# One tile pair instead of two for the keeping jobs, coarse pool waits outside the attention, and seven block products in group 0 of the second MLP

## The chip, the cores and the metric

The kernel runs on one core of a Trainium2 chip. The metric is the device time of one execution in microseconds (us); before and after are medians of several runs.

## The reference, cut to what matters

A decoder trunk of two layers on x (1 x 1024 tokens x 1024 channels, float32). Layer 0 mixes with a diagonal state-space block (S5) and a gated projection (GLU), layer 1 with 16-head stick-breaking attention over keys and values computed from the residual stream. Each layer ends with the same kind of MLP, and every sub-layer has a pre-norm whose shift, scale and gate come from a conditioning vector c:

```python
x = x + g_a[:, None, :] * mix
h = modulate(rms_norm(x, mlp_norm_g[i]), sh_m, sc_m)
ff = einsum('bsf,fd->bsd', square(relu(einsum('bsd,df->bsf', h, mlp_w1[i]))), mlp_w2[i])
x = x + g_m[:, None, :] * ff
```

with D = 1024 and D_FF = 4096. The modulations are matrix-vector products with c: `ada_chunks(c, ada_w, ada_b, n)`.

## The kernel before, in words

**Products.** Every float32 product is made from a high part (`uh`, `hi`, type fp32r) and the rest (`ul`, `lo`): three matmuls of 128x128 by 128x512, `mm3` (lines 247 to 253). A weight unit of 128x1024 is loaded by SP into one of three `raw` buffers (`load_unit`, line 209), cast to `uh` by ACT (line 217), and `ul` is the difference, on DVE (line 84 through `sub`).

**An MLP** (`mlp`, line 916) takes the 4096 hidden rows in 8 groups c of 4 blocks j. `ups` (line 1044) computes a block for both halves h of the tokens: 24 matmuls each, relu on ACT (line 927) into a tile `ra` or `rb`, the square on DVE. In group 0 the blocks are made half by half instead (lines 1052 to 1060), since the second half's norm is computed meanwhile. The way back, for one group, is done in one of two ways:
- plain (`down`, line 937): 16 outputs (8 row blocks by two halves), each 4 x 3 matmuls, 192 in all, and one DVE instruction that adds the output to x;
- seven products (`seven`, line 984): the 4 blocks by 2 halves are seen as 2x2 blocks of matrices, and for each of 4 weight units 7 products of 6 matmuls replace 8, 168 in all. `enter` (line 948) makes the right-hand combinations (T1 to T4 and three blocks as they are) with sums and splits on DVE and ACT, into `f` and `e` tiles; `blocks` (line 966) makes the left-hand ones, mostly on POOL; the results are added to x on DVE.

`fast(c)` says which way is taken: in the second MLP (layer 1) groups 1 to 7 go by seven products, group 0 plain. The first MLP is plain throughout.

**Side jobs of the GLU and of the first MLP.** `mid` (line 1635) takes 3 or 4 jobs from a list after every fourth of a down stage and after every block of an up stage. Two kinds:
- `gemv` (line 174): one 128-row piece of a modulation. SP loads 512 KB into a `raw` buffer, DVE multiplies it by silu(c) and sums (line 177, shown as CUSTOM_DVE_ANT_0). It shares the three `raw` buffers with the weights.
- `keep` (line 224): half a unit of a later weight (the output, the K/V and the query projections) is split ahead of time and put into DRAM, for the attention to load without any work. All of it is issued by POOL: load `raw` (line 231), for K/V and queries the product with the norm's scale (line 78), cast to `hi` (line 236), difference in place (line 84), two stores `kh` and `kl` (line 239). 64 jobs of 512 columns; two pairs of tiles `e` (raw, hi) are used in turn, by the half c:

```python
        while len(keeps) < 4:
            keeps.append(fs0.extra((F32, F32R)[len(keeps) % 2]))
        raw, hi = keeps[0:2] if c == 0 else keeps[2:4]
        G.dma_start(raw, src[:, cs])
```

**Order.** Side jobs are listed two gemv to one keep. The framework orders each engine's instructions with a timeline simulation when it compiles, and the engines then run them in that order, each waiting on semaphores; inside S5 and for TensorE in the attention the order is fixed by hand.

**Pools.** Tiles lie in pools that open and close along the kernel. A pool opened on bytes of closed ones has either coarse waits (each of its tiles waits for every user of those pools) or, with `reuse_waits="tile"` (`tile_pool`, line 95), waits of each tile for the users of its own bytes alone. Before, all pools opened by this helper have the fine form. Pools that land on closed ones: those after S5 (`pax0`, `fpa`, `fpe`, `gp`), `fpb` after the GLU, the attention's own (`atp`, `atk`, `aq`, `pz`, `ppt`, `ppo`, and `late`), and those after the attention (`xp1`, `raw1`, `pax1` and the second `Inner`'s).

**After the attention** the rest of its output projection runs (`oproj`, line 1672), the residual is read back into 16 `x` tiles (line 1665), and the second MLP follows to the end of the kernel.

Of the kernel before, what the change touches and what calls it, by code (L numbers as in the profile page):

```python
# [8 lines left out]
F32 = mybir.dt.float32  # L9
F32R = mybir.dt.float32r  # L10
# [4 lines left out]
PSUM = bass.MemoryType.PSUM  # L15
DRAM = bass.MemoryType.DRAM

P = 128
# [3 lines left out]
HN = 512  # L22
# [34 lines left out]
def kernel(ctx, tc, A, out):  # L57
# [4 lines left out]
    class Engine:  # L62
        def __init__(self, eng):
            self.eng = eng
# [12 lines left out]
    def mul(o, a, b, eng=V):  # L77
        eng.tensor_tensor(o, a, b, op=ALU.mult)  # L78
# [4 lines left out]
    def sub(o, a, b, eng=V):  # L83
        eng.tensor_tensor(o, a, b, op=ALU.subtract)  # L84
# [10 lines left out]
    def tile_pool(name, bufs=1, **k):  # L95
        return tc.tile_pool(name=name, bufs=bufs, reuse_waits="tile", **k)
# [6 lines left out]
    pools, turns = {}, {}  # L103

    def open_x(i):
        es = ExitStack()
        pools["x"] = es.enter_context(tile_pool(f"xp{i}", bufs=16 if i else 1))
        pools["raw"] = es.enter_context(tile_pool(f"raw{i}", bufs=3))
        es.callback(pools.pop, "raw")
        turns.clear()  # L110
        return es

    def open_ax(i):
        es = ExitStack()
        pools["ax"] = es.enter_context(tile_pool(f"pax{i}", bufs=4 if "pv" in pools else 6, space=PSUM))
        return es

    cnt = [0]
# [1 line left out]
    def nm(s):  # L120
        cnt[0] += 1
        return f"{s}_{cnt[0]}"
# [7 lines left out]
    def ps_mm(shape=(P, HN)):  # L130
        return pmm.tile(list(shape), F32, tag="mm", name=nm("pm"))

    def open_pv():
        es = ExitStack()
        pools["pv"] = es.enter_context(tile_pool("ppv", bufs=2, space=PSUM))
        es.callback(pools.pop, "pv")
        return es

# [40 lines left out]
    def ada_chunk(c0, after=None):  # L179
        def one(i):  # L180
            gemv(A["adaT"][i - 16], silr, mod[:, i:i + 1])

        def fin():
            add(mod[:, c0:c0 + 8], mod[:, c0:c0 + 8], adab[:, c0:c0 + 8])
            if after is not None:
                after()

        return [(lambda i=i: one(i)) for i in range(c0, c0 + 8)] + [fin]
# [7 lines left out]
    def queue(jobs, n, others):  # L196
        while jobs or others:
            side.extend(jobs[:n] + others[:1])
            del jobs[:n], others[:1]

    def scale_cols(n, sc0):
        stt(scl[:, 8 * n:8 * n + 8], mod[:, sc0:sc0 + 8], 1.0, gcol[:, 8 * n:8 * n + 8],
            ALU.add, ALU.mult)
# [5 lines left out]
    def load_unit(src):  # L209
        raw = raw_tile()  # L210
        SP.dma_start(raw, src)
        return split_unit(raw)
# [9 lines left out]
    kept, keeps = {}, []  # L222

    def keep(key, src, c, scale=None):
        if c == 0:
            kept[key] = [dp.tile([P, 1024], F32, name=nm(name)) for name in ("kh", "kl")]
        cs = slice(HN * c, HN * c + HN)
        while len(keeps) < 4:
            keeps.append(fs0.extra((F32, F32R)[len(keeps) % 2]))
        raw, hi = keeps[0:2] if c == 0 else keeps[2:4]  # L230
        G.dma_start(raw, src[:, cs])
        if scale is not None:
            nk = scale.shape[1] // 2
            r3 = raw.rearrange("p (k m) -> p k m", k=nk)
            mul(r3, r3, scale[:, nk * c:nk * c + nk].unsqueeze(2).broadcast_to([P, nk, HN // nk]), G)
        G.tensor_copy(hi, raw)
        sub(raw, raw, hi, G)
        for d, t in zip(kept[key], (hi.bitcast(F32), raw)):
            G.dma_start(d[:, cs], t)
# [7 lines left out]
    def mm3(ps, u, j, hl, first, last):  # L247
        uh, ul = u
        sl = slice(j * 128, j * 128 + 128)
        hi, lo = hl  # L250
        T.matmul(ps, uh[:, sl], hi, start=first, stop=False)  # L251
        T.matmul(ps, uh[:, sl], lo, start=False, stop=False)  # L252
        T.matmul(ps, ul[:, sl], hi, start=False, stop=last)  # L253
# [7 lines left out]

    def s5(hook):
        es = ExitStack()
        sp = es.enter_context(tile_pool("sp", bufs=1))
        pp = es.enter_context(tile_pool("s5ps", bufs=2, space=PSUM))

        cst = sp.tile([P, C_N], F32, name="cst")
        SP.dma_start(cst, A["cst"])
# [279 lines left out]
        class Block:  # L548
# [165 lines left out]
            pv, vt = None, None  # L714
# [163 lines left out]
    class Inner:  # L878


        def __init__(self):
            self.n, self.pools, self.es = 0, {}, {}

        def open(self, name):
            self.es[name] = ExitStack()
            self.pools[name] = self.es[name].enter_context(tile_pool("fp" + name))

        def close(self, *names):
            for name in names:
# [9 lines left out]
            return self.pools["e"].tile([P, HN], dt, tag="e", name=nm("e"), bufs=8)  # L899

        def raw(self, tag):
            return self.pools["b"].tile([P, HN], F32, tag=tag, name=nm(tag), bufs=2)

    def norm_tiles(fs):
        spare = {}

        def norm_tile(tag, bufs):
            n = spare.setdefault(tag, [0, []])
            n[0] += 1
            if len(n[1]) < bufs:  # L910
                n[1].append(fs.tile(F32))
            return n[1][(n[0] - 1) % bufs]

        return norm_tile

    def mlp(layer, xs, hs, norm, fs, mid=None, done=None, place=None):
# [3 lines left out]
        hid, raws = {}, {}  # L920

        def up(f, u, h, tag="ra"):
            p = ps_mm()
            for k in range(8):
                mm3(p, u, k, hs[k][h], k == 0, k == 7)
            r = fs.raw(tag)
            ACT.activation(r, p, AF.Relu)  # L927
            mul(r, r, r)
            return r

        def halves(r, wide=False):
            hi, lo = f_tile(wide=wide), f_tile(wide=wide)
            ACT.copy(hi, r)
            sub(lo, r, hi)
            return hi, lo
# [97 lines left out]
        def plain(c, j, h, r):  # L1033
            raws[j, h] = r
            if c and j == 0:
                return
            if c and (j, h) == (2, 0):
                hid[0, 0], hid[0, 1] = halves(raws[0, 0]), halves(raws[0, 1])
            hid[j, h] = halves(r)

        def fast(c):
            return layer == 1 and c > 0

        def ups(c, j):
            u = load_unit(w1[4 * c + j])
# [6 lines left out]
        for h in range(2):  # L1052
            for f in range(4):
                u = load_unit(w1[f])
                plain(0, f, h, up(f, u, h))
                if h == 0 and f == 0:
                    norm.rstd(1)
                elif h == 0 and f == 1:
                    norm.spread(1)
                    norm.apply(1, 0, 8)  # L1060
        for c in range(8):
# [4 lines left out]
            elif c < 7:  # L1066
                for op in range(4):
                    u = load_unit(w2[c, op])
# [5 lines left out]
            else:  # L1074
                for h in range(2):
                    for op in range(4):
                        u = load_unit(w2[c, op])
# [405 lines left out]
        return oh, ou[-2:]  # L1483


    pools["un"] = ctx.enter_context(tile_pool("unp", bufs=3))
    x_es = open_x(0)
    xall = pools["x"].tile([P, 16, HN], F32, name="xall")
    pv_es = open_pv()
    ada_es = ExitStack()  # L1490
    rowp = ada_es.enter_context(tile_pool("rowp", bufs=1))
    silr = rowp.tile([P, D], F32, name="silr")

    def gate(i):
# [27 lines left out]
    fs = fs0 = Inner()  # L1522
    fs.open("a")
    fs.open("e")
    norm = Norm(norm_tiles(fs), xs, hs, 2, M_SHM0)
    with tile_pool("gp", bufs=1) as gp:
        queue(ada_chunk(M_SHM0) + ada_chunk(M_SCM0, lambda: scale_cols(2, M_SCM0)) + ada_chunk(M_GM0), 2,
              [(lambda i=i, c=c: keep(("o", i), A["wo"][i], c)) for i in range(8) for c in range(2)])

        def glu(i, ug, uv, h):  # L1530
            ps = ps_pv if h == 1 and i <= 5 else ps_mm
            pg, pv = ps(), ps()
            for k in range(8):
                mm3(pg, ug, k, ys[k][h], k == 0, k == 7)
            if (i, h) == (6, 1):
                norm.spread(0)
                norm.apply(0, 0, 8)
            for k in range(8):
                mm3(pv, uv, k, ys[k][h], k == 0, k == 7)
            g = gp.tile([P, HN], F32, tag="g", name=nm("g"), bufs=3)  # L1540
            ACT.activation(g, pg, AF.Sigmoid)
            mul(g, pv, g)
            stt(xs[i][h], g, mod[:, M_GA0 + i:M_GA0 + i + 1], xs[i][h], ALU.mult, ALU.add)
            norm.square(i, h)

        for i in range(6):
            ug, uv = first if i == 0 else (load_unit(A["wglu"][8 + i]), load_unit(A["wglu"][i]))
            for h in range(2):
                glu(i, ug, uv, h)
                if i == 0:  # L1550
                    for c in range(1 + 3 * h, 4 + 4 * h):
                        gate(c)
            if i:
                pump(9)
        for h in range(2):
            for i in range(6, 8):
                ug = load_unit(A["wglu"][8 + i])
                uv = load_unit(A["wglu"][i])
                glu(i, ug, uv, h)
            if h == 0:  # L1560
                norm.rstd(0)
# [100 lines left out]
    for h in range(2):  # L1662
        for k in range(8):
            xs2[k][h] = xt()
            SP.dma_start(xs2[k][h], xd[k][h])
    fs = Inner()
    for name in "aeb":
        fs.open(name)
        ctx.enter_context(fs.es[name])
# [117 lines left out]
```

## Time and profile before

| | us |
|---|---|
| median of 3 runs | 2519.15 |
| lowest, highest run | 2518.10, 2522.58 |
| the profiled execution | 2516.43 |
| its span, first to last instruction | 2514.7 |
| TensorE (PE) busy | 2350.6 (93%) |
| VectorE (DVE) busy | 1754.3 (70%) |
| GpSimd (POOL) busy | 909.5 (36%) |

The profiled execution lies 2.7 us below the median. The stages in the span: S5 to about 240 us, the GLU to about 410, the first MLP to about 1130, the attention to about 1793, the rest of its projection and the second MLP to the end. PE is the TensorE matmul row; a single matmul is shown longer than the distance to the next one, since they overlap, so a stage's matmuls are counted and divided into its time. An answer with "<-" names what ended an idle time.

### The profile page before, as it was taken

How to read it: one execution, taken by the hardware profiler on the slowest of the kernel's cores; microseconds unless marked ns; L12 is line 12 of the kernel's file. 1: busy time of each engine (PE TensorE's matmuls, PEld its weight loads, DVE VectorE, ACT ScalarE, POOL GpSimd, SP SyncE). 2: the span in 40 equal slices, each digit the busy share in tenths (PEclk: the TensorE clock that was granted, in tenths of full speed). 3: DMA queues.
4: the chain of work that ended last, by engine and by line, in shares of the span. 5: the costliest groups of instructions: out<-in, count | busy, mean ns of one | idle time of the engine just before them, and what ended most of it. 6: DMA issues, size and time to landing. Idle time of an engine off the chain costs nothing.

```text
span 2514.7 us, 33271 instructions
## 1 busy us (share of the span) xinstructions
PE 2350.6 (93%) x12552; PEld 1979.3 (79%) x12552; DVE 1754.3 (70%) x2570; ACT 941.8 (37%) x1710; POOL 909.5 (36%) x965
## 2 busy tenths in 40 slices
PE   3888999989999999999899999998999999999998
PEld 2677788867778888888888888887778888888886
DVE  7997557766776545345687877788583667876787
ACT  5653124211111222133566666676351232223221
POOL 4664460378775000014333323343110322342334
PEclk8899999999999999998999999999999999999999
DMA  4225863667766333123211111126721011111112
GB/s 150 86 79 188 283 221 105 216 241 251 252 239 217 101 117 126 45 89 102 81 58 39 64 68 68 59 100 213 250 78 57 34 51 59 60 42 51 56 54 76
DMA packets 105344, 297.08 MB, mean 118 GB/s; under 512 B 13280, under 2 KB 25568, under 8 KB 105184
## 3 DMA queue, kind: packets, MB, share of 16 engines
q1 hardware_dynamic: 87264, 240.42, 27.9%
q0 software_dynamic: 15360, 50.34, 5.5%
q10 hardware_dynamic: 2560, 4.20, 0.7%
q8 instruction: 99, 1.62, 0.3%
q14 instruction: 61, 0.50, 0.1%
HBM read 241.23 MB, written 49.48 MB: 116 GB/s over the span
## 4 chain that ended last, share of the span: by engine, by line
PE 61%; DVE 17%; DMA 11%; issue 5%; ACT 2%; POOL 1%; SPq 0%; DVEq 0%; POOLq 0%; ACTq 0%
DMA raw<-in_adaT_dram 8%; PE pm L70 8%; PE pm L251 8%; PE pm L252 8%; PE pm L253 8%; PE pa L1001 3%; PE pa L999 3%; PE pa L1000 3%; PE pt L70 3%; DVE sn L1282 3%; DVE raw L177 2%; PE pa L253 2%; PE pa L251 2%; PE pa L252 2%; PE po L70 2%
## 5 line engine op out<-in xcount | busy, mean ns | idle before, releaser
L251 PE MATMUL pm<-h,uh 128*128 128x512 f32 x1192 | 465.6, 393 | 19.3 <-ACT rb L927 15.8
L253 PE MATMUL pm<-h,ul 128*128 128x512 f32 x1192 | 465.5, 391 | 4.7 <-DVE ul L84 4.7
L252 PE MATMUL pm<-h,uh 128*128 128x512 f32 x1192 | 466.3, 391 | 1.6 <-DVE h L93 1.6
L217 ACT CAST uh<-raw 128x1024 fp32r<-128x1024 f32 x130 | 136.7, 1051 | 486.9 <-PE pa L252 154.5
L84 DVE TENSOR_TENSOR ul<-raw,uh 128x1024 fp32r<-128x1024 f32 (+1 forms) x158 | 202.7, 1283 | 126.5 <-ACT uh L217 103.8
L251 PEld LDWEIGHTS pm<-h,uh 128*128 128x128 f32 x1192 | 225.0, 189 | 71.5 <-ACT rb L927 19.3
L177 DVE CUSTOM_DVE_ANT_0 raw<-raw,silr 128x1024 f32<-128x1024 f32 x119 | 162.5, 1369 | 155.4 <-DMA raw<-in_adaT_dram 140.6
L253 PEld LDWEIGHTS pm<-h,ul 128*128 128x128 f32 x1192 | 225.1, 189 | 52.5 <-DVE ul L84 5.6
L252 PEld LDWEIGHTS pm<-h,uh 128*128 128x128 f32 x1192 | 225.3, 189 | 48.6 <-DVE h L93 2.2
L70 PE MATMUL pm<-uh,h 128*128 128x256 f32 x1024 | 238.5, 301 | 3.8 <-DVE rs L1138 3.0
L1282 DVE TENSOR_TENSOR_SCAN sn<-sn 128x768 f32<-128x768 f32 (+7 forms) x128 | 180.6, 1417 | 46.5 <-ACT sn L1277 45.2
L81 POOL TENSOR_TENSOR f<-f,f 128x512 f32<-128x512 f32 x30 | 44.0, 1468 | 397.3 <-ACT f L831 397.2
L70 PEld LDWEIGHTS pm<-uh,h 128*128 128x128 f32 x1024 | 181.7, 199 | 5.0 <-DVE rs L1138 3.4
L81 POOL TENSOR_TENSOR raw<-raw 128x256 f32<-128x256 f32 x28 | 26.0, 929 | 411.4 <-DVE ul L84 411.4
L251 PE MATMUL pa<-f,uh 128*128 128x512 f32 x396 | 154.4, 390 | 1.7 <-DVE xall L93 1.0
L252 PE MATMUL pa<-f,uh 128*128 128x512 f32 x396 | 154.1, 389 | 0.0
L253 PE MATMUL pa<-f,ul 128*128 128x512 f32 x396 | 153.7, 389 | 0.0
L70 PE MATMUL pm<-ul,h 128*128 128x256 f32 x512 | 148.7, 290 | 0.9 <-DMA ul<-kl 0.9
L78 POOL TENSOR_TENSOR sg<-sg,sn 128x512 f32<-128x512 f32 x64 | 93.0, 1453 | 122.5 <-DVE sn L1282 56.3
L70 PE MATMUL pm<-h,uh 128*128 128x512 f32 x402 | 133.7, 414 | 0.0
L93 DVE SCALAR_TENSOR_TENSOR x<-pa,mod,x 128x512 f32<-128x512 f32 x143 | 103.3, 743 | 43.5 <-PE pa L253 29.6
L1277 ACT ACTIVATE sn<-z,rrr 128x512 f32<-128x512 f32 (+1 forms) x192 | 111.6, 581 | 46.9 <-PE z L70 45.4
(380 smaller groups left out, 5497.7 us busy)
## 6 DMA issues: line engine op xcount, KB each, us to landing
raw<-in_w_dram SPq DMA_DIRECT2D x140, 512.0 KB, 3.3
raw<-in_adaT_dram SPq DMA_DIRECT2D x96, 512.0 KB, 3.7
uh<-kh SPq DMA_DIRECT2D x40, 512.0 KB, 4.2
ul<-kl SPq DMA_DIRECT2D x40, 512.0 KB, 4.0
kh<-e POOLq DMA_DIRECT2D x64, 256.0 KB, 2.7
kl<-e POOLq DMA_DIRECT2D x64, 256.0 KB, 3.6
raw<-in_wT_dram SPq DMA_DIRECT2D x24, 512.0 KB, 4.3
raw<-in_wglu_dram SPq DMA_DIRECT2D x20, 512.0 KB, 4.7
```

The lines of the kernel that those rows point to most:

```text
L70: return lambda *a, **k: tc.keep_in_program_order(f(*a, **k))
L78: eng.tensor_tensor(o, a, b, op=ALU.mult)
L84: eng.tensor_tensor(o, a, b, op=ALU.subtract)
L93: V.scalar_tensor_tensor(o, a, s, b, op0=op0, op1=op1)
L177: V.tensor_tensor_reduce(raw, raw, row, 1.0, 0.0, op0=ALU.mult, op1=ALU.add, accum_out=bcol)
L217: ACT.copy(uh, raw)
L251: T.matmul(ps, uh[:, sl], hi, start=first, stop=False)
L252: T.matmul(ps, uh[:, sl], lo, start=False, stop=False)
L253: T.matmul(ps, ul[:, sl], hi, start=False, stop=last)
L999: T.matmul(p, uh[:, sl], hi, start=(i == 0), stop=False)
L1277: ACT.activation(g[:, HN * hb + c0:HN * hb + HN], p[:, c0:], AF.Sigmoid, scale=pj.rr[:, 2, t, a:a + 1])
L1282: V.tensor_tensor_scan(g[:, s0:], g[:, s0:], g[:, s0:], 1.0, op0=ALU.mult, op1=ALU.bypass)
```

## The change

1. `keep` uses one pair of tiles for all jobs.
2. All pools but the attention's (`atp`, `atk`, `aq`, `pz`, `ppt`, `ppo`, `late`) get the coarse waits: `tile_pool(...)` becomes `tc.tile_pool(name=..., ...)`.
3. `fast` is true for all groups of layer 1. Group 0's blocks go through `enter`, in the order of group 0 (four blocks of the first half, then four of the second), and so all eight `ra`/`rb` tiles are alive at once: the second `Inner` gets 4 buffers for each of the two tags.

```diff
-        while len(keeps) < 4:
-            keeps.append(fs0.extra((F32, F32R)[len(keeps) % 2]))
-        raw, hi = keeps[0:2] if c == 0 else keeps[2:4]
+        if not keeps:
+            keeps.extend((fs0.extra(F32), fs0.extra(F32R)))
+        raw, hi = keeps
         G.dma_start(raw, src[:, cs])
...
-        pools["x"] = es.enter_context(tile_pool(f"xp{i}", bufs=16 if i else 1))
-        pools["raw"] = es.enter_context(tile_pool(f"raw{i}", bufs=3))
+        pools["x"] = es.enter_context(tc.tile_pool(name=f"xp{i}", bufs=16 if i else 1))
+        pools["raw"] = es.enter_context(tc.tile_pool(name=f"raw{i}", bufs=3))
...
-        pools["ax"] = es.enter_context(tile_pool(f"pax{i}", bufs=4 if "pv" in pools else 6, space=PSUM))
+        pools["ax"] = es.enter_context(tc.tile_pool(name=f"pax{i}", bufs=4 if "pv" in pools else 6, space=PSUM))
...
-        def __init__(self):
+        def __init__(self, raws=2):
+            self.raws = raws
...
-            self.pools[name] = self.es[name].enter_context(tile_pool("fp" + name))
+            self.pools[name] = self.es[name].enter_context(tc.tile_pool(name="fp" + name, bufs=1))
...
-            return self.pools["b"].tile([P, HN], F32, tag=tag, name=nm(tag), bufs=2)
+            return self.pools["b"].tile([P, HN], F32, tag=tag, name=nm(tag), bufs=self.raws)
...
         def fast(c):
-            return layer == 1 and c > 0
+            return layer == 1
...
                 u = load_unit(w1[f])
-                plain(0, f, h, up(f, u, h))
+                if fast(0):
+                    enter(f, h, up(f, u, h, "ra" if f < 2 else "rb"))
+                else:
+                    plain(0, f, h, up(f, u, h))
...
-    fs = Inner()
+    fs = Inner(4)
```

The pools `ppv`, `sp`, `s5ps`, `unp`, `rowp` and `gp` change like `raw`.

## Rows read from the trace of the kernel before

**Rows 1.** Page, part 1: busy time, share and instructions of each engine.

```profile
PE 2350.6 (93%) x12552; PEld 1979.3 (79%) x12552; DVE 1754.3 (70%) x2570; ACT 941.8 (37%) x1710; POOL 909.5 (36%) x965
```

**Rows 2.** Table by stretch: length, then each engine's busy time and instructions, clock, DMA.

```profile
474.00:800.00 326.00, 306.41 (x1321) 248.58 (x1320) 225.48 (x255) 54.88 (x77) 249.22 (x286) 0.98 0.71 248
800.00:1090.00 290.00, 290.00 (x1297) 240.71 (x1296) 137.88 (x187) 62.93 (x87) 0.00 (x0) 1.00 0.28 95
1900.00:1943.00 43.00, 43.00 (x192) 35.61 (x191) 17.42 (x21) 4.65 (x5) 0.00 (x0) 1.00 0.14 50
1990.00:2080.00 90.00, 90.00 (x399) 74.55 (x398) 67.82 (x91) 24.31 (x36) 31.92 (x28) 1.00 0.16 53
520.00:540.00 20.00, 13.53 (x55) 10.76 (x54) 13.62 (x17) 2.06 (x3) 15.93 (x18) 0.83 0.73 256
```

**Rows 3.** 474 to 800 us: the chain of waits by line, and who waited.

```profile
by line: DMA raw<-in_adaT_dram 49.6%; DVE raw L177 14.5%; DVE ul L84 10.7%; issue 10.0%; DVE xall L93 4.1%; DVE f L84 3.2%; DVE ra L78 1.8%; DVE rb L78 1.2%; ACT f L933 1.2%; DVE mod L177 0.6%; PE pa L251 0.6%; PE pa L252 0.6%; PE pa L253 0
...
DVE raw L177 <- DMA raw<-in_adaT_dram: 86.1, 44, 3.9
...
PE pm L251 <- ACT rb L927: 15.8, 7, 6.5
```

**Rows 4.** DVE groups of instructions: three of 474 to 800 us, three of 900 to 1090.

```profile
L177 DVE CUSTOM_DVE_ANT_0 raw<-raw,silr 128x1024 f32<-128x1024 f32 x54 | 79.6, 1474 | 86.1 <-DMA raw<-in_adaT_dram 86.1
L84 DVE TENSOR_TENSOR ul<-raw,uh 128x1024 fp32r<-128x1024 f32 x27 | 43.7, 1620 | 0.0
L78 DVE TENSOR_TENSOR rb<-rb 128x512 f32<-128x512 f32 x12 | 15.8, 1317 | 0.0
...
L84 DVE TENSOR_TENSOR ul<-raw,uh 128x1024 fp32r<-128x1024 f32 x18 | 22.0, 1224 | 33.3 <-ACT uh L217 32.8
L177 DVE CUSTOM_DVE_ANT_0 raw<-raw,silr 128x1024 f32<-128x1024 f32 x9 | 10.8, 1223 | 6.7 <-DMA raw<-in_wT_dram 5.1 <-ACT silr L1571 1.7
L78 DVE TENSOR_TENSOR rb<-rb 128x512 f32<-128x512 f32 x9 | 6.2, 688 | 12.0 <-ACT rb L927 12.0
```

**Rows 5.** Page, part 6: DMA issues, KB each, median us from issue to landing.

```profile
raw<-in_w_dram SPq DMA_DIRECT2D x140, 512.0 KB, 3.3
raw<-in_adaT_dram SPq DMA_DIRECT2D x96, 512.0 KB, 3.7
...
kl<-e POOLq DMA_DIRECT2D x64, 256.0 KB, 3.6
```

**Rows 6.** POOL's groups of instructions, 474 to 800 us (the keeping jobs).

```profile
L84 POOL TENSOR_TENSOR e<-e,e 128x512 f32<-128x512 f32 x48 | 63.3, 1318 | 1.2
L78 POOL TENSOR_TENSOR e<-e,scl 128x512 f32<-128x512 f32 x48 | 62.8, 1309 | 108.0 <-DVE scl L93 71.6 <-DMA e<-in_wkv_dram 24.6 <-DMA e<-in_wq_dram 11.2
L236 POOL CAST e<-e 128x512 fp32r<-128x512 f32 x48 | 48.4, 1011 | 2.8
```

**Rows 7.** The load of a keeping job (line 231): issue to landing, min/median/max.

```profile
DMA to landing us min/median/max: 2.8/3.6/6.5
```

**Rows 8.** POOL in order of time: first scaled keep, last store, next work.

```profile
474.36 3.43 POOL L78 TENSOR_TENSOR e<-e,scl 128x512 f32<-128x512 f32 x2 [71.62 <-DVE scl L93]
...
795.71 0.54 POOL L239 DMA_DIRECT2D kl<-e  x1
1104.41 1.74 POOL L81 TENSOR_TENSOR f<-f,f 128x512 f32<-128x512 f32 x1 [308.16 <-ACT f L831]
```

**Rows 9.** End of the attention in order of time: SP's queue, then PE.

```profile
1781.35 1.28 SPq L211 DMA_DIRECT2D raw<-in_w_dram  x3
...
1795.38 9.78 SPq L1665 DMA_DIRECT2D x<-xd  x16
...
1792.95 0.39 PE L251 MATMUL pa<-h,uh 128*128 128x512 f32 x1
```

**Rows 10.** PE's waits from 1790 us to the end.

```profile
PE pa L251 <- DVE x L93: 2.9, 1, 2.9
PE pa L999 <- ACT e L933: 2.6, 2, 2.0
```

More of the change, by code (lines that the diff above doesn't have):

```diff
@@ L134, in open_pv @@
         es = ExitStack()
-        pools["pv"] = es.enter_context(tile_pool("ppv", bufs=2, space=PSUM))
+        pools["pv"] = es.enter_context(tc.tile_pool(name="ppv", bufs=2, space=PSUM))
         es.callback(pools.pop, "pv")
@@ L263, in s5 @@
         es = ExitStack()
-        sp = es.enter_context(tile_pool("sp", bufs=1))
-        pp = es.enter_context(tile_pool("s5ps", bufs=2, space=PSUM))
+        sp = es.enter_context(tc.tile_pool(name="sp", bufs=1))
+        pp = es.enter_context(tc.tile_pool(name="s5ps", bufs=2, space=PSUM))
         cst = sp.tile([P, C_N], F32, name="cst")
@@ L1483, in attention @@
         return oh, ou[-2:]
-    pools["un"] = ctx.enter_context(tile_pool("unp", bufs=3))
+    pools["un"] = ctx.enter_context(tc.tile_pool(name="unp", bufs=3))
     x_es = open_x(0)
@@ L1490 @@
     ada_es = ExitStack()
-    rowp = ada_es.enter_context(tile_pool("rowp", bufs=1))
+    rowp = ada_es.enter_context(tc.tile_pool(name="rowp", bufs=1))
     silr = rowp.tile([P, D], F32, name="silr")
@@ L1525 @@
     norm = Norm(norm_tiles(fs), xs, hs, 2, M_SHM0)
-    with tile_pool("gp", bufs=1) as gp:
+    with tc.tile_pool(name="gp", bufs=1) as gp:
         queue(ada_chunk(M_SHM0) + ada_chunk(M_SCM0, lambda: scale_cols(2, M_SCM0)) + ada_chunk(M_GM0), 2,
```

## The prediction, made before the change was run

> **What bounds the kernel now.** I read the page's busy times first, then the table by stretch, then chain and waits of the stretch in which PE was not full. PE is busy for 93% of the span and nothing else is near it [rows 1]; the table says where that holds [rows 2]. In the second MLP it holds exactly: 399 matmuls in 90 us without a gap, 225.6 ns each, and group 0's plain way back is 192 matmuls in 43.0 us. From 800 to 1090 us, in the first MLP, it holds too: 1297 matmuls in 290 us, 223.6 ns each. But from 474 to 800 us, in the same kind of work, PE makes 1321 matmuls in 326 us. At 225.6 ns they need 298 us, so some 28 us are lost there, in stalls such as that of 520 to 540 us (55 matmuls where 89 fit, granted clock 0.83). The chain of this stretch runs hardly through PE at all: half of it is the loading of gemv rows, a third is DVE [rows 3]. DVE waits 86.1 us for those rows in 44 waits, and PE shows 15.8 us of waiting for the relu into rb; the rest of its 28 us is shorter gaps and the lower clock. So this stretch is bound by DVE, which runs its queue in order: a gemv that waits for its load holds up the squares and splits that PE needs.
>
> What sets the stretch apart is the keeping jobs: their first scaled product starts at 474.4 us and their last store goes out at 795.7 [rows 8], and POOL is busy 249 of the 326 us, then 0 of 290 [rows 2]. While they run, DVE's instructions are longer [rows 4]: the gemv 1474 ns against 1223, the weight split 1620 against 1224, the square 1317 against 688. A gemv row takes 3.7 us to land where a weight takes 3.3 [rows 5].
>
> **The change, part by part.**
>
> *Group 0 by seven products.* 24 matmuls fewer, at 225.6 ns [rows 2]: **-5.4 us**, all on PE's path, as PE has no gap in that stage. DVE gets more work: in a steady group, seven products and the next blocks together, it is busy 67.8 of 90 us and PE does not wait [rows 2], while in group 0's plain stage it is busy 17.4 of 43; so the additions to x and POOL's left-hand blocks (POOL 31.9 of 90 in a steady group) are covered by PE. What is new is the order at the start: both columns of right-hand blocks become ready one block (5.4 us) apart, some ten DVE instructions of 0.69 us each [rows 4] and six casts beside them, 14 us for both, with three weight splits and two squares 19 us. Until the product that needs the last of them PE has 5.4 us of the last block, 10.8 us of the next group's first block and 2.7 us of products: 18.9 us. So it just fits. The nearest row for it not fitting is the last group, where no next block covers the splits, and PE waits 2.6 us for the cast into e [rows 10]. Bounds 0 and +3, I take **+1**, as most of the cover is there. The 4 buffers of ra and rb let a relu start earlier; PE waits for no relu in this MLP's full stretches, so 0.
>
> *Coarse pool waits.* They matter only for work that now starts before all users of the closed pools are done. After S5 that is the first keeping load; it may then start later, and costs nothing, as POOL sits idle 71.6 us before the scaled jobs anyway [rows 8]. After the attention [rows 9]: three w1 loads go out at 1781.35, but are needed only once the second MLP begins, behind all x tiles and projections: 0. The x tiles are read from 1795.38, which is after the attention's last split already: 0. The first oproj matmuls into `pa` start at 1792.95; they would now wait for the last copy out of the attention's PSUM, about 1 us. Behind them on PE are the rest of the projections, and the 2.9 us that PE waits for DVE later in that stage [rows 10] swallow it. Should the w1 loads come among those of x on SP's queue, the projection's weights are later by three loads of 512 KB, 3.3 us for one alone [rows 5]; bounds 0 and +4. I take **+0.5**.
>
> *One pair for the keeping jobs.* Now each load waits on POOL until the store of the job before has landed. A job is then a chain: load 3.6 [rows 7], product 1.3, cast 1.0, difference 1.3 [rows 6], one store issue 0.5 [rows 8], the second store 3.6 [rows 5], with some 0.3 us between them 11.7; as waiting loads are the slow ones I take 12.0 (11.4 to 12.5). Before, 48 jobs took 321 us, 6.7 each, two overlapping. So they run from 474 to 474 + 48 x 12.0 - 3.6 = 1047 us (1018 to 1071). Queued behind POOL's waits is nothing but the jobs themselves until 1104, when the sums for the next norm begin [rows 8]; in the GLU stage, where 16 unscaled jobs share POOL with the norm's sums, those can be held up for one job, and ACT's next square with them; no row prices that, 0 to +2, I take 0 because PE is full there and the sums are a block apart.
>
> The gain: in 326 us only 27 of the 48 jobs run, 21 (44%) move behind 800 us. The longer DVE instructions cost now: gemv 54 x 0.25 = 13.6 us, weight splits 27 x 0.40 = 10.7, and some 50 squares and splits at up to 0.63, 31: at most 55 us [rows 4]. 44% is 24 us, and about half of DVE's busy time (the DVE lines are 36% of 326 us, 116 of 225) is on the chain [rows 2, 3]: 12 us. Of the loads, 0.4 us (3.7 against 3.3) in 44 waits is 18 us, 44% is 8. Together 20 of the 28 us lost. The 21 jobs that come later lengthen DVE's work by as much, where DVE is busy 137.9 of 290 us [rows 2]; most is covered, but there are gemv rows behind 800 us too [rows 4], so I take back 4, for **-16**. Bounds: all 28 at one end; at the other nothing, with up to +8 of new stalls behind 800 us.
>
> Here a rule speaks against me. The Trainium skill, page "SBUF — State Buffer", section "Who interferes with whom", says that a DVE instruction with two SBUF inputs and a GpSimd instruction that reads SBUF exclude each other for their whole length. By that the time which DVE loses hangs on the number of POOL instructions and stays the same 55 us, only moved, and if DVE stayed the bound to 1047 us the sum would be 0 from this part. By the rows it is not the bound behind 800 us.
>
> **Sum**, against the profiled execution of 2516.4 us (span 2514.7, with 1.7 around it): -5.4 + 1 + 0.5 - 16 = -20, 2496.5. It lies 2.7 below the median of the runs; on the median's scale **2499**.
>
> **Rivals.**
> 1. *The relief does not come.* The gemv stream stays the bound, because the jobs now also lie beside the gemv rows behind 800 us, and what the first groups win the later ones lose. For it: DVE's waits for loads are the larger part (86 us) and the landing changes by only 0.4 us. Against it: from 800 us on, without the jobs, PE has no gap at all. Time: -5.4 + 1.5 = -4, 2515 (to 2519 with the upper bounds). The Trainium skill, page "Perfetto Trace Analysis", section "Identifying the Most-Contended Engine", would lead here as well, with its advice to work on the engine with the highest occupancy, as only the 24 matmuls touch it.
> 2. *The full relief.* PE-bound throughout: -28 - 4 = 2487. For it: the jobs' pace falls below half, and PE has no stalls where POOL is idle. Against: what is left of the overlap.
> 3. *Slower: the keeping chain runs too long.* If a job takes over (1088 + 3.6 - 474.4)/48 = 12.9 us (1088 being 1104 less the 16 gained), the last jobs stand before the sums for the next norm on POOL, and behind these come the norm's statistics on PE and the attention's first K/V block. At 13.5 us the jobs end at 1119, 31 us late, less the 20: +11, 2530. For it: single landings of 6.5 us [rows 7]. Against: the median of the same row.
>
> **How the numbers follow.** Forecast 0.55, rival 1 0.2, rival 2 0.12, rival 3 0.08, and 0.05 for another order out of the planner that costs more than the gains. The range reaches from rival 2 to rival 1 with its bounds, 2486 to 2519, and leaves out rival 3 and the planner. About 0.2% (5 us) is what a measurement of this kernel tells from no change. Faster: forecast, rival 2 and a quarter of rival 1, 0.72; same: most of rival 1, 0.15; slower 0.13.
>
> **What would show it.** 168 matmuls of the seven-product lines more and 192 plain ones fewer, and no PE gap over 2 us near group 0; keeping jobs of about 12 us from 474 to near 1047 us; squares and weight splits of DVE shorter before 800 us; PE near 89 matmuls per 20 us from 500 to 760; the same stretch's chain back on PE. I am wrong if PE still loses over 15 us there, if gaps of PE appear behind 800 us, or if POOL's norm sums stand behind keeping jobs at the end of the first MLP.

## The result, and the profile after

The changed kernel takes **2493.7 us** (median of 4 runs, 2491.5 to 2496.6) against 2518.6 for the kernel before beside it: ratio 0.9900, 95% interval 0.9882 to 0.9917, some 25 us or 1.0% faster. Forecast were 2499, within 2486 to 2519. The execution profiled took 2496.6 us, the slowest of the four, so the two profiles differ by 20 us only.

Busy time of each engine, from the page of the changed kernel:

```profile
PE 2341.2 (94%) x12528; PEld 1973.2 (79%) x12528; DVE 1765.3 (71%) x2612; ACT 944.0 (38%) x1720; POOL 944.1 (38%) x989
```

The 24 matmuls are gone [rows 1]. The table by stretch of the changed kernel, columns as in [rows 2]:

```profile
474.00:800.00 326.00, 316.12 (x1376) 259.95 (x1375) 197.08 (x266) 58.73 (x81) 141.78 (x163) 0.98 0.59 203
800.00:1090.00 290.00, 288.51 (x1289) 239.18 (x1288) 151.49 (x180) 62.79 (x87) 112.55 (x125) 1.00 0.42 147
520.00:540.00 20.00, 15.75 (x63) 12.59 (x62) 11.21 (x15) 3.18 (x5) 6.60 (x8) 0.91 0.54 187
720.00:740.00 20.00, 20.00 (x90) 16.57 (x89) 13.29 (x19) 5.24 (x8) 6.88 (x9) 1.00 0.52 175
1870.00:1940.00 70.00, 70.00 (x310) 57.74 (x309) 62.56 (x80) 21.07 (x32) 28.64 (x24) 1.00 0.17 58
```

From 474 to 800 us PE makes 1376 matmuls where it made 1321. Full, at 225.6 ns, it would make 1445; so (1445 - 1376) x 0.2256 = 15.6 us are still lost, of 28.0 before. The stall of 520 to 540 us is smaller, but there. Behind 800 us PE makes 8 matmuls fewer than before, 1.8 us. Group 0's seven products (they lie in 1870 to 1940) run without a gap.

POOL in order of time shows the slower keeping jobs [rows 8]: 48 of them in 563 us, 11.7 each.

```profile
473.15 1.98 POOL L78 TENSOR_TENSOR e<-e,scl 128x512 f32<-128x512 f32 x1 [49.24 <-DVE scl L93]
...
1036.34 0.54 POOL L239 DMA_DIRECT2D kl<-e  x1
...
1092.68 1.72 POOL L81 TENSOR_TENSOR f<-f,f 128x512 f32<-128x512 f32 x1 [55.80 <-ACT f L831]
```

DVE's groups of instructions, 474 to 800 us of the changed kernel: they are shorter than in [rows 4] (DVE is busy 197.1 us, 225.5 before), but more of the stretch goes into waiting for gemv rows (112.0 us, 86.1 before), so DVE did not become free to the extent that POOL did.

```profile
L177 DVE CUSTOM_DVE_ANT_0 raw<-raw,silr 128x1024 f32<-128x1024 f32 x55 | 72.8, 1323 | 112.0 <-DMA raw<-in_adaT_dram 112.0
L84 DVE TENSOR_TENSOR ul<-raw,uh 128x1024 fp32r<-128x1024 f32 x30 | 37.6, 1255 | 3.6 <-ACT uh L217 3.6
L78 DVE TENSOR_TENSOR rb<-rb 128x512 f32<-128x512 f32 x14 | 12.1, 864 | 0.5 <-ACT rb L928 0.5
```

PE's waits from 1770 us to the end: the 2.6 us of the last group [rows 10] are no longer in the list, the wait for x is halved, and the wait for the last copy out of the attention's PSUM is new.

```profile
PE pa L251 <- DVE x L93: 1.4, 1, 1.4
...
PE pa L251 <- DVE o L81: 0.9, 1, 0.9
```

Two stretches tell the parts apart in every profile: **A**, from the first product into pv in the first MLP (2.3 us behind the first down product, from which the expectations count) to POOL's first norm sum; **B**, from the first projection matmul into pa to the end. In the nine profiles in which nothing of B's code differs (after, e1, e5 to e10, e12) B reads 710.9 to 714.2, and A differs by 5.7 us between e2 and e11, which are the same up to there: smaller differences between single profiles say nothing. Lost is what PE lost in 474 to 800, worked out as above; the ratio is to the kernel before, measured beside each run.

| kernel | ratio (95%) | A, us | B, us | matmuls in 474 to 800, lost us |
|---|---|---|---|---|
| before | 1 | 633.3 | 721.7 | 1321, 28.0 |
| after | 0.9900 (0.9882 to 0.9917) | 622.9 | 711.0 | 1376, 15.6 |
| e1 two pairs | 0.9965 (0.9951 to 0.9980) | 636.8 | 712.0 | 1306, 31.4 |
| e2 one pair alone | 0.9938 (0.9922 to 0.9954) | 617.9 | 721.5 | 1389, 12.6 |
| e3 plain group 0 | 0.9919 (0.9902 to 0.9936) | 622.8 | 716.1 | 1369, 17.1 |
| e4 fine waits | 0.9886 (0.9869 to 0.9903) | 620.3 | 714.7 | 1378, 15.1 |
| e5 no jobs | 0.9816 (0.9794 to 0.9838) | 608.9 | 711.2 | 1436, 2.0 |
| e6 transfers only | 0.9969 (0.9952 to 0.9986) | 641.5 | 711.1 | 1293, 34.3 |
| e7 arithmetic only | 0.9883 (0.9862 to 0.9904) | 622.3 | 710.9 | 1375, 15.8 |
| e8 fourth raw | 0.9991 (0.9978 to 1.0004) | 613.5 | 714.2 | 1435, 2.3 |
| e9 three per step | **0.9843** (0.9830 to 0.9857) | 608.9 | 712.9 | 1430, 3.4 |
| e10 fourth raw, late | 0.9965 (0.9953 to 0.9976) | 616.8 | 711.8 | 1395, 11.3 |
| e11 one pair, four buffers | 0.9926 (0.9913 to 0.9939) | 623.6 | 718.1 | 1369, 17.1 |
| e12 two pairs, three per step | 0.9922 (0.9908 to 0.9937) | 628.8 | 711.2 | 1347, 22.1 |

A ratio's 0.1% is 2.5 us. The expectations call the gemvs "modulation products".

### The profile page after: what moved, and what is told of

Its sections match the earlier page's. It is cut to its first block, busy times and chain, and to the rows that moved or that the text cites. A ratio compares the mean times of both kernels' runs of the same rounds, so it can differ in the third digit from the quotient of the medians.

```text
span 2494.8 us, 33310 instructions
## 1 busy us (share of the span) xinstructions
PE 2341.2 (94%) x12528; PEld 1973.2 (79%) x12528; DVE 1765.3 (71%) x2612; ACT 944.0 (38%) x1720; POOL 944.1 (38%) x989
## 5 line engine op out<-in xcount | busy, mean ns | idle before, releaser
L177 DVE CUSTOM_DVE_ANT_0 raw<-raw,silr 128x1024 f32<-128x1024 f32 x119 | 157.5, 1326 | 175.8 <-DMA raw<-in_adaT_dram 162.1
L84 DVE TENSOR_TENSOR ul<-raw,uh 128x1024 fp32r<-128x1024 f32 (+1 forms) x158 | 191.0, 1209 | 121.8 <-ACT uh L217 95.8
L78 POOL TENSOR_TENSOR sg<-sg,sn 128x512 f32<-128x512 f32 x64 | 93.0, 1453 | 121.9 <-DVE sn L1286 62.9
L78 POOL TENSOR_TENSOR e<-e,scl 128x512 f32<-128x512 f32 x48 | 62.8, 1307 | 199.9 <-DMA e<-in_wkv_dram 98.2
L251 PE MATMUL pa<-f,uh 128*128 128x512 f32 x332 | 129.4, 390 | 0.3 <-DVE xall L93 0.3
L252 PE MATMUL pa<-f,uh 128*128 128x512 f32 x332 | 129.2, 389 | 0.0
L253 PE MATMUL pa<-f,ul 128*128 128x512 f32 x332 | 128.8, 389 | 0.0
L84 DVE TENSOR_TENSOR wt<-pt,wt 128x512 fp32r<-128x512 f32 (+1 forms) x160 | 100.7, 630 | 37.5 <-ACT wt L1314 30.2
```

Of the source, the lines that this page charges most:

```text
L177: V.tensor_tensor_reduce(raw, raw, row, 1.0, 0.0, op0=ALU.mult, op1=ALU.add, accum_out=bcol)
```

## The experiments

**The parts one by one: e1 to e4.** e1 is the changed kernel with two pairs of tiles again:

```diff
-        if not keeps:
-            keeps.extend((fs0.extra(F32), fs0.extra(F32R)))
-        raw, hi = keeps
+        while len(keeps) < 4:
+            keeps.append(fs0.extra((F32, F32R)[len(keeps) % 2]))
+        raw, hi = keeps[0:2] if c == 0 else keeps[2:4]
```

> The changed kernel with two pairs of keeping tiles put back; the rest as changed. Theory (the single pair slows the keeping jobs from 6.7 to 11.7 us each and so takes POOL and DMA work out of 474 to 800 us): 11 to 16 us slower than the changed kernel, about 2506 us, with the first norm sum on POOL back at about 1104 us and some 28 us of PE lost again in 474 to 800. Rival (the single pair did nothing, the first MLP moved for another reason such as another order of instructions or the pools' waits): within 3 us of the changed kernel's 2494.

e1 is 0.65% slower than the changed kernel, 16 us, just beyond the theory's range, with POOL's norm sum at 1107.5 us and 31 us lost. The rival falls.

e2 is the same edit the other way round, made to the kernel before.

> The kernel before with the single pair alone. Theory: 11 to 16 us faster than before, 2503 to 2508 us, the first norm sum on POOL at about 1092 us, and everything after the attention as before (about 707 us from the x reload to the end). Rival (the parts need each other, or the gain lies all in the second MLP): within 3 us of 2518.

0.62% faster than the kernel before, 15.6 us, and B unchanged. So the pair is worth 16 us with or without the other parts.

In e3 group 0 is plain again:

```diff
-            return layer == 1
+            return layer == 1 and c > 0
```

> The changed kernel with group 0 of the second MLP computed plainly again, its 24 matmuls back, the second Inner's four buffers kept. Theory (24 matmuls of 225.6 ns and nothing else): 5.4 us slower than the changed kernel, about 2499.5 us. Rival 1 (the seven products also set off what took the other 4 us after the attention, the order of the work and the stall in the last group): 8 to 11 us slower, about 2503.5, with the stall of 2.6 us back at the end. Rival 2 (the split chain costs what the matmuls save): within 2 us.

0.19% slower than the changed kernel (4.8 us, though the intervals overlap), and B is 5.1 us longer: the 24 matmuls. In e3 the last group's stall stays away, so group 0's products are not what removed it.

e4 goes back to the finer waits at all ten places where the change made them coarse; the instructions are those of the changed kernel, in the same order on DVE, ACT and POOL.

> The changed kernel with the finer waits put back on every pool, the instruction order the same. Theory (the coarse waits cost some 0.5 us at the seams): 0 to 1 us faster, no difference that can be measured. Rival (the coarse waits delay the second MLP's start by several us): 2 to 4 us faster.

No difference that can be measured (0.9886 beside 0.9900). What the coarse waits do at the seam shows in PE's waits: the wait for the last copy out is in the changed kernel's list and not in e4's, and e4 has the x wait at its old length.

```profile
PE pa L251 <- DVE x L93: 2.9, 1, 2.9
```

In the profiles with coarse waits the x wait is 1.3 to 2.9 us long, with fine ones 2.6 to 2.9; but the new wait of 0.9 comes on top, so that both together are 2.2 to 3.8 us. A gain or loss of a us cannot be settled here.

**The last group: e11.** It is e2 with `self.raws` and `Inner(4)` for the second MLP taken from the change, so four `ra` and `rb` buffers in place of two.

> The kernel before with the single pair and with four ra and rb buffers in the second MLP, group 0 plain, the finer waits everywhere. Read against e2_one_pair_alone, from the first output projection's matmul to the end, 721.5 us there and 716.1 in e3_plain_group0, which has the coarse waits too. Theory (the four buffers remove the stall of 2.6 us in the last group, the coarse waits the rest): 718 to 720 us, the wait for the last reload 2.9 us as before. Rival 1 (the buffers are all of it): 716 us. Rival 2 (they do nothing, the coarse waits all): 721 us, with the stall of 2.6 us still there.

The stall of 2.6 us in the last group, still in e2, is gone (a wait of 1.0 us for `rb` is new there), and B goes from 721.5 to 718.1. Cleaner than B is the count of matmuls in 75 us that end 5 us before the end: 300 in the kernel before and in e2, 312 in e11 and in every other profile with four buffers, so 12 x 0.2256 = 2.7 us; part of it is the granted clock, 0.98 in e2's stretch and 1.00 in e11's. The theory held as far as the buffers go. How they do it is not shown: with them DVE and ACT also run in another order, from 1940 us on. The seven products' 5.1 and these 2.7 leave 2.9 of B's 10.7 us, within its scatter.

The stretch of 75 us in e2, then PE's waits from 1740 us in e2:

```profile
2416.40:2491.40 75.00, 70.67 (x300) 56.57 (x298) 55.49 (x75) 16.99 (x27) 29.45 (x24) 0.98 0.16 60
```

```profile
PE pa L999 <- ACT e L933: 2.6, 2, 2.0
```

The stretch in e11:

```profile
2422.00:2497.00 75.00, 72.18 (x312) 57.66 (x310) 58.84 (x80) 18.02 (x28) 30.28 (x24) 1.00 0.16 61
```

**Why the jobs cost PE time: e5 to e7.** All three have two pairs, like e1, and are read against it. e5 leaves out all jobs but the first two:

```diff
...
+        if len(kept) > 1:
+            return
...
```

> The changed kernel with two pairs, all keeping jobs but the first two left out (the kept halves of every other weight are missing, so the attention reads wrong weights). Read against e1_two_pairs, from the first down product of the first MLP to the first norm sum on POOL, which took 635.6 us in the kernel before and 639.1 us with two pairs. Theory (POOL's arithmetic and the jobs' transfers together cost 20 of the 28 us that PE loses in 474 to 800; the last 8 are the modulation products' own loads): 616 to 620 us. Rival (the products' own loads and DVE work are the limit): over 630 us.

e6 leaves out the jobs' arithmetic:

```diff
...
-            mul(r3, r3, scale[:, nk * c:nk * c + nk].unsqueeze(2).broadcast_to([P, nk, HN // nk]), G)
-        G.tensor_copy(hi, raw)
-        sub(raw, raw, hi, G)
-        for d, t in zip(kept[key], (hi.bitcast(F32), raw)):
+            mul(raw[:, 0:nk], raw[:, 0:nk], scale[:, nk * c:nk * c + nk], G)
+        for d, t in zip(kept[key], (raw, raw)):
```

> Two pairs, the jobs' loads and stores kept, their POOL arithmetic left out but for one multiply of a few columns that keeps the start at the scale (both stored halves are the raw weight, unscaled, so the attention reads wrong weights). Theory (12 of the 20 us come from POOL's arithmetic lengthening DVE's, 8 from the loads): DVE's modulation product back at 1.22 us beside the transfers, its loads still late, 624 to 631 us for the stretch that took 639.1. Rival 1 (transfers are all of it): 636 us or more, for they come faster one after the other here. Rival 2 (arithmetic is all of it): 616 to 620 us, as without jobs.

e7 leaves out their transfers:

```diff
...
-        G.dma_start(raw, src[:, cs])
...
-        for d, t in zip(kept[key], (hi.bitcast(F32), raw)):
-            G.dma_start(d[:, cs], t)
+        if len(kept) == 1:
+            for d, t in zip(kept[key], (hi.bitcast(F32), raw)):
+                G.dma_start(d[:, cs], t)
```

> Two pairs, the POOL arithmetic of all jobs kept, their loads and stores left out but for the first weight's (it works on a constant; the attention reads wrong weights). Theory: the arithmetic runs without gaps, some 3.7 us a job, DVE's modulation product is lengthened to 1.5 us or more while it runs, the landing of its loads goes back towards 3 us; 12 of the 20 us are left, 627 to 632 us for the stretch. Rival 1 (transfers are all of it): 616 to 620 us. Rival 2 (arithmetic is all of it): 636 us or more.

474 to 800 us by stretch and DVE's gemv group, first e1, with complete jobs:

```profile
474.00:800.00 326.00, 304.37 (x1306) 247.59 (x1305) 222.48 (x252) 54.67 (x76) 250.67 (x286) 0.97 0.72 244
```

```profile
L177 DVE CUSTOM_DVE_ANT_0 raw<-raw,silr 128x1024 f32<-128x1024 f32 x54 | 85.7, 1588 | 91.9 <-DMA raw<-in_adaT_dram 91.9
```

e5:

```profile
474.00:800.00 326.00, 325.44 (x1436) 269.21 (x1435) 178.45 (x265) 63.27 (x89) 0.00 (x0) 1.00 0.41 136
```

```profile
L177 DVE CUSTOM_DVE_ANT_0 raw<-raw,silr 128x1024 f32<-128x1024 f32 x53 | 65.0, 1226 | 110.3 <-DMA raw<-in_adaT_dram 110.3
```

e6:

```profile
474.00:800.00 326.00, 305.25 (x1293) 248.79 (x1292) 165.49 (x247) 54.08 (x75) 93.77 (x184) 0.96 0.73 245
```

```profile
L177 DVE CUSTOM_DVE_ANT_0 raw<-raw,silr 128x1024 f32<-128x1024 f32 x54 | 66.2, 1225 | 148.1 <-DMA raw<-in_adaT_dram 148.1
```

e7:

```profile
474.00:800.00 326.00, 316.40 (x1375) 259.48 (x1374) 219.89 (x265) 59.22 (x82) 199.42 (x142) 0.99 0.41 136
```

```profile
L177 DVE CUSTOM_DVE_ANT_0 raw<-raw,silr 128x1024 f32<-128x1024 f32 x55 | 80.6, 1466 | 83.8 <-DMA raw<-in_adaT_dram 83.8
```

Without jobs PE loses 2 us: the loss needs the jobs, the gemv rows alone do not make it, and a wait of 110 us on DVE costs nothing there. With transfers alone (46 jobs in the stretch, nearly the 48 of before) DVE's instructions are as short as without jobs, and yet PE loses as much as with complete jobs. With arithmetic alone DVE's instructions are as long as before (54 us more busy time than in e6), and PE loses 15.8. So the two do not add up, 34 and 16 alone but 31 together. These are not shares of a price, as each part alone also runs faster than in the whole job: e6's last store goes out at 740 us, 799 in e1, and e7's last difference ends at 673. Why they do not add can be read from e1 and e6: with the arithmetic DVE is busy 57 us longer (222.5 against 165.5) and waits 56 us less for gemv rows (91.9 against 148.1). The time by which arithmetic lengthens DVE's instructions is taken, for the most part, from waiting that is there anyway. My theory of 12 + 8 falls in both halves. In the expectations' count (A and 2.3 us) e5 reads 611.2, below even the theory, e6 643.8, as its first rival said, and e7 624.6, between its first rival and the theory.

**Would earlier loads help? e8 and e10.** Both are the changed kernel in which every second gemv loads into a buffer `gr` of its own; in e10 the buffer is opened only behind the gated layer (the GLU).

```diff
-        raw = raw_tile()
+        turns["g"] = turns.get("g", -1) + 1
+        raw = (pools["gr"].tile([P, 1024], F32, tag="gr", name=nm("gr"))
+               if "gr" in pools and turns["g"] % 2 == 0 else raw_tile())
```

> The changed kernel, every second modulation product loading into a fourth raw buffer of its own in place of the ring of three. Theory (the 15 us of PE that are still lost in 474 to 800 come from DVE waiting for these loads, 112 us in 49 waits, because a load can only be issued when a buffer is free): DVE's waits for them fall by a third or more, PE loses 8 us or less there, 4 to 9 us faster than the changed kernel, 2485 to 2490. Rival (the loads are late by the DMA rings' own time, however early they are issued): the same DVE waits, within 2 us of 2494.

The theory had the loss in 474 to 800 us right (1435 matmuls) and the kernel wrong: 23 us slower than the changed one by the ratios. The gemvs ran ahead into the gated layer (52 of them between 230 and 474 us, 34 in the changed kernel), and the first product into pv came at 500.3 us in place of 469.8. Only 38 were left for 474 to 800, in place of 55, so the full PE there does not show that earlier loads help. By stretch, e8:

```profile
230.00:450.00 220.00, 196.89 (x833) 157.60 (x832) 132.50 (x200) 51.22 (x74) 83.19 (x94) 0.95 0.73 243
474.00:800.00 326.00, 325.05 (x1435) 268.90 (x1434) 187.83 (x242) 68.32 (x92) 135.72 (x162) 1.00 0.53 178
```

> The fourth raw buffer of e8, opened only after the gated layer, so that no product runs ahead into it. Theory 1 (e8 was slow only because 22 more products ran in 230 to 450, and the loads are late for want of a buffer): 230 to 450 as in the changed kernel, PE's loss in 474 to 800 under 5 us, 4 to 10 us faster, 2484 to 2490. Theory 2 (it is the traffic that counts; a fourth buffer lets more products run early in 474 to 800 and only moves the loss): more than 55 products in 474 to 800, the loss there 8 us or more, within 3 us of 2494 or slower.

Neither theory as it stands: by the ratios e10 is 16 us slower than the changed kernel. A is 6 us shorter, hardly more than the scatter, but the first product into pv comes at 487.0 us in place of 469.8. Between 230 and 490 us PE waited for DVE's `h` (9.2 us) and `ul` (4.4). 37 gemvs ran up to 474 us, three more than in the changed kernel; whether these alone hold DVE up was not tried and stays open.

**The spacing: e9 and e12.** e9 is the changed kernel with one line changed:

```diff
-        pump((3, 4)[cyc[0] % 2])
+        pump(3)
```

> The changed kernel, three side jobs at every step of the first MLP in place of three and four in turn, so that the modulation products last to the end of that MLP. Theory after e5 to e8 (the traffic in 474 to 800, not POOL's arithmetic, sets what PE loses there, and thinner traffic loses less): some 6 products fewer in 474 to 800, PE's loss there 3 to 7 us in place of 9.9 beside the clock, 3 to 7 us faster than the changed kernel, 2487 to 2491. Rival 1 (the loss moves with the products into 800 to 1090): within 2 us of 2494. Rival 2 (products left over at the end hold up the last group): 2 to 6 us slower.

e9 beats both kernels: **0.9843, 2483.5 us**, 14 us under the changed kernel by the ratios, more than expected. PE's loss in 474 to 800 us is 3.4 us in place of 15.6, and A equals that of e5, without any jobs. And the traffic and the waits are hardly less: DMA share 0.59 as in the changed kernel, 51 gemvs in place of 55, each waited for 110.1/51 = 2.16 us on average (112.0/55 = 2.04 in the changed kernel). By stretch, e9:

```profile
474.00:800.00 326.00, 324.60 (x1430) 267.69 (x1429) 196.02 (x258) 62.66 (x86) 144.40 (x167) 1.00 0.59 196
800.00:1090.00 290.00, 290.00 (x1297) 240.68 (x1296) 160.79 (x197) 64.73 (x90) 114.44 (x125) 1.00 0.49 166
```

```profile
L177 DVE CUSTOM_DVE_ANT_0 raw<-raw,silr 128x1024 f32<-128x1024 f32 x51 | 69.0, 1353 | 110.1 <-DMA raw<-in_adaT_dram 110.1
```

The code queues two gemvs and one job in turn, so a step of three side jobs takes two gemvs, while a step of four can take three. The timeline of the changed kernel shows what a gemv more can do, at the stall of 520 to 540 us: PE waits 4.3 us. ACT has the relu into rb done at 516.8 us; DVE is still to do two gemvs before rb's square, and the second waits 4.58 us for its row. So the square starts at 527.63, ACT's cast of it at 529.18, and the next relu, which PE needs, is queued behind that cast and one of a weight. PE's wait from 515 to 545 us, then DVE and ACT in order of time:

```profile
PE pm L251 <- ACT rb L928: 4.3, 1, 4.3
```

```profile
517.55 1.22 DVE L177 CUSTOM_DVE_ANT_0 raw<-raw,silr 128x1024 f32<-128x1024 f32 x1 [1.02 <-DMA raw<-in_adaT_dram]
...
526.48 1.23 DVE L177 CUSTOM_DVE_ANT_0 raw<-raw,silr 128x1024 f32<-128x1024 f32 x1 [4.58 <-DMA raw<-in_adaT_dram]
527.63 0.08 DVE L177 DVE_READ_ACCUMULATOR2_ANT mod<- 128x1 f32 x1
527.63 1.52 DVE L78 TENSOR_TENSOR rb<-rb 128x512 f32<-128x512 f32 x1
```

```profile
516.20 0.60 ACT L928 ACTIVATE rb<-pm 128x512 f32<-128x512 f32 x1 [4.61 <-PE pm L253]
529.18 0.62 ACT L934 CAST f<-rb 128x512 fp32r<-128x512 f32 x1 [12.38 <-DVE rb L78]
```

In e9 there are two gemvs less ahead of that square (11 in place of 13 since the square before), and it starts at 524.81:

```profile
523.36 1.51 DVE L177 CUSTOM_DVE_ANT_0 raw<-raw,silr 128x1024 f32<-128x1024 f32 x1 [4.33 <-DMA raw<-in_adaT_dram]
524.81 0.08 DVE L177 DVE_READ_ACCUMULATOR2_ANT mod<- 128x1 f32 x1
524.81 1.77 DVE L78 TENSOR_TENSOR rb<-rb 128x512 f32<-128x512 f32 x1
```

The changed kernel's longest wait of PE in 474 to 800 us, 4.8 us before 643.3, has the same form. Between 520 and 800 us it stands at the only place between two squares of an up stage where DVE has two gemvs to do; at all others, and at all in e9, it has at most one. Both rows come late, the square of `ra` starts at 641.41, ACT's cast of it at 642.12 and the relu that PE needs at 642.64. DVE in order of time:

```profile
633.63 1.23 DVE L177 CUSTOM_DVE_ANT_0 raw<-raw,silr 128x1024 f32<-128x1024 f32 x1 [3.04 <-DMA raw<-in_adaT_dram]
...
638.35 1.91 DVE L177 CUSTOM_DVE_ANT_0 raw<-raw,silr 128x1024 f32<-128x1024 f32 x1 [2.87 <-DMA raw<-in_adaT_dram]
...
641.41 0.68 DVE L78 TENSOR_TENSOR ra<-ra 128x512 f32<-128x512 f32 x1
```

Three at every step is also fewer jobs a step (3 in place of 3.5 on average) and leaves 4 gemvs fewer in 474 to 800 us. Four at every step was not tried, so the runs do not part the evenness from the smaller number.

> e9 (three side jobs at every step) with two pairs of keeping tiles. Theory (both the jobs' pace and the products' spacing make VectorE late at the end of a group's down products, and each has its own share): the jobs end near 800 us again, PE loses some 8 to 16 us in 474 to 800 where e9 lost none, 6 to 14 us slower than e9, 2490 to 2498. Rival 1 (the spacing was all of it; with three a step the pace of the jobs does not matter): within 3 us of e9's 2483.5, and the single pair was needed only for the uneven steps. Rival 2 (the pace is most of it): 2500 or more.

0.9922: 20 us slower than e9 (above the theory's 6 to 14, and its second rival's side), 11 us faster than e1. The jobs did not end near 800 us: the last store goes out at 873, so steps of three also slow the jobs where two pairs would let them run faster, and the 11 us are not the spacing of the gemvs alone. With one pair the last store stays where it was (1037 in e9, 1036 in the changed kernel). So both parts have a share, with the other part either way: the single pair 16 us at steps of three and four, 20 at steps of three; steps of three 11 us with two pairs, 14 with one.

## Why the prediction was right, and where it was not

*Group 0, -5.4 + 1.* Right: B shrinks by 5.1 between e3 and the changed kernel. The +1 did not come; PE has no gap from 1870 to 1940 us.

*"The 4 buffers ... PE waits for no relu in this MLP's full stretches, so 0."* Failed: -2.7 (e11). I looked at full stretches only; in the last group, which I had cited as a bound [rows 10], no next block covers the splits, and there the buffers took this stall away.

*Coarse waits, +0.5.* The new wait is there with 0.92 us, and is swallowed as forecast, and the wait behind it is 1.4 us in place of 2.9. Over the whole kernel no difference can be measured (e4): right within what can be told.

*One pair, -16.* The size is right (-15.6 in e2, -16.4 against e1), the jobs' pace too (11.7 us for 12.0, last store at 1036 for 1047). The working behind the size failed in two steps. "DVE part 12, loads 8" is not how it comes about: transfers alone make the whole loss (e6), arithmetic alone half (e7), and they overlap. And the 8 us that I left as the gemv rows' own go with the jobs as well (e5). That the sum came out is in part luck. It stood at 20 won before 800 us and 4 given back behind it; by the counts of matmuls 12.4 are won before 800 in the changed kernel's profile, 15.4 in e2 and 15.8 against e1, and behind 800 the changed kernel gives back 1.8 and e2 nothing. Both terms were too large, and they make up for each other.

*The signs.* By my own signs I was not wholly right: PE still loses 15.6 us in 474 to 800, where over 15 was to count against me (15.1 in e4, 12.6 in e2), it makes 63 matmuls and not 89 in 520 to 540, and a wait of 1.5 us stands behind 800, at 893 (none in e2 and e4). What I had not seen is that the loss also hangs on how many gemvs a step takes: e9, with the same pair and three jobs a step, loses 3.4. The other signs came as forecast: the matmuls, the jobs, the shorter squares and weight splits, no gap over 2 us near group 0, and the norm sums free of the jobs. Whether the stretch's chain is back on PE cannot be read, as the chain of the changed kernel reaches back only to 1865 us.

*The rule against it* (the Trainium skill, page "SBUF — State Buffer", section "Who interferes with whom"): that POOL's arithmetic lengthens DVE's two-input instructions is what e6 and e7 show side by side (gemv 1225 and 1466 ns). That the sum would therefore be 0 does not follow, as DVE's lengthened time lies largely in its waits. Nor was the lengthening only moved: for the same 2612 instructions DVE is busy 1785.8 us with two pairs (e1), 1765.3 with one (the changed kernel) and 1722.9 without jobs (e5), so the single pair took away 20.5 of 62.9 us. Page lines of e1 and e5:

```profile
PE 2341.6 (93%) x12528; PEld 1971.3 (79%) x12528; DVE 1785.8 (71%) x2612; ACT 944.0 (38%) x1720; POOL 943.2 (38%) x989
```

```profile
PE 2330.3 (94%) x12528; PEld 1967.6 (80%) x12528; DVE 1722.9 (70%) x2612; ACT 944.1 (38%) x1720; POOL 632.6 (26%) x631
```

*Rivals.* Rival 1 (no relief) falls with e1 and e2. Rival 2 (full relief, 2487) did not come from the change, though e9 reached it with one line more. Rival 3 had its margin: the last job ended 56 us ahead of the norm sums.

*The sum* was -20 and measured -25 by the ratio (21 to 30 by its interval): about 3 of the 5 us are the buffers, and 1 the chain that cost nothing. Rival 1's upper end was added up wrongly: with the bounds +3 and +4 in place of +1.5 it is 2521, not 2519.

## What to carry to other kernels

An in-order engine that does side work between pieces of the main chain is judged by the worst moment, not by its mean: here 112 us of waiting cost 16 us of TensorE in one spacing of the side jobs, and 110 us cost 3 in another, at the same DMA share. Before work is taken away or slowed down, look at how many side jobs are queued ahead of the instruction that the chain needs at each step, and hold the largest of these numbers down. And when two costs run beside each other, leave out each in turn before you add them up: here a lengthened instruction and a late load on one queue did not add.

## What the runs showed of the hardware

The median landing of the gemv rows, 3.7 us before [rows 5], is 4.2 on the page of the changed kernel, which is faster; a median landing time did not tell whether PE waits. POOL's own instructions do not have one length either: the difference, 1318 ns in [rows 6], takes 1401 in the changed kernel, 1501 in e9 and 1790 in e7, where the jobs have no gaps; what sets it was not tried:

```profile
L84 POOL TENSOR_TENSOR e<-e,e 128x512 f32<-128x512 f32 x48 | 85.0, 1790 | 0.0
```

And a stall of PE costs more than its length: in the changed kernel a wait of 4.3 us at 520 to 540 us leaves 63 matmuls where 89 fit, 5.9 us, with the granted clock of that stretch at 0.91.
